# Turning the first quarter of the next norm's rows with a transposing DMA instead of TensorE, at the end of three feed-forward blocks

## The chip, the cores and the metric

The kernel runs on one core of a Trainium2 chip. The metric is device time in microseconds (us) of one execution, the median of several runs. The profile is of one further execution, taken by the hardware profiler.

## The reference

A two-layer encoder over 512 tokens with 1024 channels, float32 throughout. Each layer is a half-step feed-forward block, a mixer, and a second half-step feed-forward block; a final norm follows.

```python
def swiglu(x, w_in, w_out):
    gu = x @ w_in
    g, u = jnp.split(gu, 2, axis=-1)
    return (jax.nn.silu(g) * u) @ w_out
...
    for l in range(DEPTH):
        x = x + 0.5 * swiglu(rms_norm(x, ffn1_norm[l]), ffn1_w_in[l], ffn1_w_out[l])
        x = x + mixer(rms_norm(x, mix_norm[l]), mix_w_in[l], mix_gate_bias[l], na_rpb[l],
                      na_w_out[l], f_w_out[l], mix_w_o[l])
        x = x + 0.5 * swiglu(rms_norm(x, ffn2_norm[l]), ffn2_w_in[l], ffn2_w_out[l])
    return rms_norm(x, final_norm)
```

`D_FF` is 2816. The mixer is neighbourhood attention and a 2-D Fourier transform, gated and summed; the change does not touch it.

## The kernel before

The residual `x` stays in SBUF with tokens on the partitions: 4 blocks of 128 tokens by 1024 channels. Every matrix product is made in split precision: each operand is written as a high part (`whi`, `xh`, `c1h`, ...) and a low remainder (`wlo`, `xl`, `c1l`, ...), and three matmuls replace one: high by high (line 508 of `late_low`), low activation by high weight (line 509), and high activation by low weight (line 511). The high part is an ACT copy, the low part a DVE subtraction that needs that copy: `split` (lines 321 and 322) does this for activations, `Item.prep` (lines 191 and 194) for weights. The products of a block are arranged in Strassen's manner, with seven products numbered m = 1 to 7, so that sums of weight blocks are wanted as well as the blocks themselves.

**Weights.** They come from DRAM as granules of 128 by 1024 float32 (512 KB). `Raw.load` issues the load on SP's queue (line 148) into one of 9 buffers named `raw`; where a sum of two granules is wanted, either a second DMA on GpSimd's queue adds the other granule to it on the way (line 150, `accum_op`), or DVE adds two resident granules (`summed`, line 164). A `raw` buffer comes free once its `wlo` is written. `whi` and `wlo` have three buffers each; `Stream` prepares two granules ahead of the one in use and fetches eight ahead.

**The end of a feed-forward block.** `stage_ffn` first makes the gated hidden activations, turns them to channel-major tiles `at`, and then goes through the output product in 21 steps, i = 0 to 20: m = 1 for three chunks c of the hidden width (i = 0 to 2), m = 2 (i = 3 to 5), then m = 5, 6, 7, 3 for c = 0 (i = 6 to 9), for c = 1 (i = 10 to 13) and for c = 2 (i = 14 to 17), then m = 4 (i = 18 to 20). A step has two weight granules and 18 (c = 0) or 24 matmuls of 512 columns into tiles named `o`. `make(i)` prepares a step's activations: for m = 5, 6, 7 and 4 a DVE combination of two `at` tiles (line 750), then `split`. Step i calls `make(i + 1)` before its product and `make(i + 2)` behind it. At the last chunk of an m, `update` (line 756, DVE) adds the product to `x`, and `squares` (line 375, ACT) sums the squares for the next norm.

**The next norm's rows.** The next stage wants `x` turned: channels on partitions, in high and low parts `xh` and `xl`, plus the gained raw values `xr`. This is done in four quads (i, j): i is the half of the channels, j the half of the tokens. `Norm.quad` does one of them: eight TensorE transposes of 128 by 128 into two PSUM tiles `tr` (line 413), four ACT copies out of PSUM that apply the norm's gain (line 416), one ACT copy for the high part (line 417) and one DVE subtraction for the low part (line 418). Quad (0, 0) is called at step i = 6, once m = 2 has finished that quarter of `x`; the quads (1, 1) and (0, 1) follow at i = 18. This holds for the three feed-forward blocks that are not the last one. The next stage begins with quad (0, 0).

**The other way to turn.** The gated activations are turned without TensorE: `apart` copies a float32 tile as two planes of 16-bit words (`zs`, two ACT copies, line 346) and issues one transposing DMA `zt <- zs` on SP's queue (line 347); `joined_words` puts the words together again (two ACT copies, line 356). Tiles `zs`, `zt`, `xr`, `at` and the split activations share one pool, `slot`, of 23 buffers of 4 KB per partition.

Each engine executes its instructions in order. The order in which instructions go to each queue comes from a scheduler at build time that follows the program's order as priority; only where the code says `manual_schedule` is it the written one. Steps i = 6 to 17 are not under such a block.

Of the kernel before, what the change touches and what calls it, by code (L numbers as in the profile page):

```python
# [9 lines left out]
F32 = mybir.dt.float32  # L10
# [4 lines left out]
AF = mybir.ActivationFunctionType  # L15
# [5 lines left out]
T = 512  # L21
# [69 lines left out]
def encoder_kernel(  # L91
# [3 lines left out]
    V, S, G, PE = nc.vector, nc.scalar, nc.gpsimd, nc.tensor  # L95
# [11 lines left out]
    def nm(s):  # L107
        uid[0] += 1
        return f"{s}_{uid[0]}"

    def slot(dt=F32, s="k", shape=(4, 256)):
        return kp.tile([P, *shape], dt, tag="k", name=nm(s), bufs=23)
# [8 lines left out]
    def pair(s="ps"):  # L121
        return [bank(s), bank(s)]


    x = cp.tile([P, TB, D], F32, tag="x", name="x")
# [146 lines left out]
    class Stream:  # L272
# [32 lines left out]
        def next(self, ahead=AHEAD):  # L305
            self.prep(self.pos + 1 + ahead)
            it = self.items[self.pos]
            self.pos += 1
            return it.out

    ws = Stream()
# [7 lines left out]
    def split(hi, lo, src, scale=None):  # L319
        if scale is None:  # L320
            S.activation(hi, src, AF.Copy)
            V.tensor_tensor(lo, src, hi.bitcast(F32), ALU.subtract)
            return
        S.activation(hi, src, AF.Copy, scale=scale)
        V.scalar_tensor_tensor(lo, src, scale, hi.bitcast(F32), ALU.mult, ALU.subtract)
# [15 lines left out]
    def apart(z):  # L341

        s, t = slot(U16, "zs", (2, 4, 2, P)), slot(U16, "zt", (2, 4, 256))
        words = z.bitcast(U16).rearrange("p b (q f h) -> p h q b f", q=4, h=2)
        for h in range(2):
            S.activation(s[:, h], words[:, h], AF.Copy)  # L346
        nc.sync.dma_start_transpose(
            out=t.rearrange("p h q (b t) -> p (h q b) t", b=2), in_=s.rearrange("p h q b f -> p (h q b f)")
        )
        return t  # L350

    def joined_words(to, t):

        to = to.bitcast(U16).rearrange("p i (t w) -> p w i t", w=2)
        for w in range(2):
            S.activation(to[:, w], t[:, w], AF.Copy)  # L356

    class Norm:
# [39 lines left out]

        def quad(self, i, j):
            self.quad_high(i, j)()  # L400

        def quad_high(self, i, j):

            self.tiles(i)
            js = slice(j * 256, (j + 1) * 256)
            hq, lq = self.h[i][:, :, js], self.l[i][:, :, js]
            raw = self.raw[i, j] = slot(F32, "xr")
            for k2 in range(2):
                tr = bank("tr").rearrange("p (a b) -> p a b", a=2)
                for k in range(2):  # L410
                    d = (4 * i + 2 * k2 + k) * P
                    for b in range(2):
                        PE.transpose(tr[:, k, b * P : (b + 1) * P], x[:, 2 * j + b, d : d + P], ident)
                for k in range(2):
                    kt = 2 * k2 + k
                    S.activation(raw[:, kt, :], tr[:, k, :], AF.Copy, scale=self.gain(4 * i + kt))
            S.activation(hq, raw, AF.Copy)
            return lambda: V.tensor_tensor(lq, raw, hq.bitcast(F32), ALU.subtract)
# [156 lines left out]
    def snap(ps):  # L575
        t = slot(F32, "sn", (2, T))
        for b in range(2):
            S.activation(t[:, b, :], ps[b], AF.Copy)  # L578
        return t
# [35 lines left out]
    def stage_ffn(norm, nxt, late):  # L615
# [25 lines left out]
        raw = norm.raw  # L641
# [24 lines left out]
        if first:  # L666
            for g in range(2):
                w = ws.next()
# [103 lines left out]
        def make(i):  # L772
            if i < len(steps) and i not in made:
                m, c, f = steps[i]
                made[i] = hl(f(), c, f"c{m}")
# [95 lines left out]
        for jb in range(0 if first else 1, NB):  # L871
            f0 = 2 + 4 * jb
            if first and jb == 0:
                with tc.manual_schedule(engines={mybir.EngineType.DVE, mybir.EngineType.Activation}):
                    pa = pair("A")
                    product(pa, acts[1], K4, True)
                    for j in range(2):
                        t = snap(pcl[j])
# [39 lines left out]
        for i, (m, c, _) in enumerate(steps):  # L918
            make(i)
            if i:  # L920
                make(i + 1)
            key = {6: 1, 4: 7}.get(m, m)
            if key not in ps:
                ps[key] = pair(f"o{key}")
            if m == 4 and c == 0 and nxt.mix:
                make(i + 2)
                ws.finish_stage()
                swap_pools(1)
            product(
                ps[key], made.pop(i), list(range(len(CHUNK[0][c]))), c == 0 and m in (1, 2, 3, 5, 7), c == 2,  # L930
                m in (4, 6), by_block=late and i == len(steps) - 1,
            )
            if i == 0:
                settle_at()
            if i == 2:
                turned.reverse()
                joined()
            if i == 5:
                joined()
            if m == 4 and c == 0 and not late:  # L940
                with tc.manual_schedule(engines={mybir.EngineType.DVE, mybir.EngineType.Activation}):
                    make(i + 2)
                    nxt.quad(1, 1)
                    if nxt.mix:
                        nxt.low01 = nxt.quad_high(0, 1)
                    else:
                        nxt.quad(0, 1)
            make(i + 2)
            if i == 6 and not late:
                nxt.quad(0, 0)  # L950
            if m == 4 and c == 1:
                update(ps[1], 1, 0, 1)
            if m == 4 and c == 0 and late:
                gf[0] = slot(F32, "gf", (D,))
                nc.sync.dma_start(out=gf[0], in_=bass.AP(tensor=gfin.tensor, offset=gfin.offset, ap=[[0, P], [1, D]]))
            if c < 2:
                continue
            if m == 1:
                update(ps[1], 0, 0, -1)
            elif m == 2:  # L960
                update(ps[2], 0, 0, 1)
                nxt.squares(0, 0)
            elif m == 5:
                update(ps[5], 0, 1, 1)
                update(ps[5], 1, 1, -1)
            elif m == 6:
                update(ps[1], 1, 1, 1)
            elif m == 7:
                update(ps[7], 1, 1, 1)
                nxt.squares(1, 1)  # L970
                update(ps[1], 0, 1, -1)
            elif m == 3:
                update(ps[3], 0, 1, 1)
                nxt.squares(0, 1)
                if late:
                    make(i + 3)
            elif late:
                with (
                    tc.issue_after(ws.items[-1].last.ins),
                    tc.manual_schedule(engines={mybir.EngineType.DVE, mybir.EngineType.Activation}),  # L980
                ):
                    ready = nxt.inverses(2)
                    next(ready)
                    gained(2, 0)
                    next(ready)
                    gained(2, 1)
                    for _ in ready:
                        pass
                    scaled(nxt, 2)
                    update(ps[7], 1, 0, 1, (0,))  # L990
                    nxt.squares(1, 0, (0,))
                    root = [nxt.inverse(b, *nxt.terms(b)) for b in range(2)]
                    next(root[0])
                    gained(3, 0)
                    gained(3, 1)
                    scaled(nxt, 3)
                    update(ps[7], 1, 0, 1, (1,))
                    nxt.squares(1, 0, (1,))
                    next(root[1])
                    next(root[0])  # L1000
                    gained(0, 0)
                    next(root[0])
                    gained(0, 1)
                    scaled(nxt, 0)
                    next(root[1])
                    next(root[1])
                    whole(nxt, 1, 0)
                    whole(nxt, 1, 1)
            else:
                update(ps[7], 1, 0, 1)  # L1010
                if not nxt.mix:
                    nxt.squares(1, 0)
                nxt.later((1, 0))
# [797 lines left out]
    def swap_pools(kind, fetch=True):  # L1811

        if scope[0]:
            scope[0].close()
        scope[0] = ExitStack()
        name = nm("stage")
        scope_pool[0] = scope[0].enter_context(tc.tile_pool(name=name, bufs=1, reuse_waits="tile"))
        if kind:
            mix_pool[0] = scope_pool[0]
            raw_pool[0] = mix_raw  # L1820
        else:
            raw_pool[0] = ffn_raw
        if fetch:
            ws.enter(ws.stage + 1)
# [16 lines left out]
    for l in range(L):  # L1841
        nxt = Norm(3 * l + 1)
        stage_ffn(norm, nxt, False)
        norm, nxt = nxt, Norm(3 * l + 2)
        stage_mixer(l, norm, nxt)
        norm, nxt = nxt, Norm(3 * l + 3)
# [141 lines left out]
```

## Time and profile before

| | us |
|---|---|
| three runs | 1858.61, 1860.62, 1858.87 |
| median | 1858.87 |
| the profiled execution | 1859.64 |
| its span, first to last instruction | 1857.9 |

Between the span and the execution's own time lie 1.7 us, before the first and behind the last instruction. TensorE's granted clock was 0.999 of full speed. The profile names matmuls PE and weight loads into the array PEld; a matmul's end is modelled and overlaps the next one's start, so the distance between starts (0.227 us for 512 columns) says more than a matmul's own duration (0.389 us).

The output products of the three blocks that the change touches begin at 220.6, 821.7 and 1142.2 us of the trace and are called block A, B and C below.

### The profile page before, as it was taken

How to read it: one execution, taken by the hardware profiler on the slowest of the kernel's cores; microseconds unless marked ns; L12 is line 12 of the kernel's file. 1: busy time of each engine (PE TensorE's matmuls, PEld its weight loads, DVE VectorE, ACT ScalarE, POOL GpSimd, SP SyncE). 2: the span in 40 equal slices, each digit the busy share in tenths (PEclk: the TensorE clock that was granted, in tenths of full speed). 3: DMA queues.
4: the chain of work that ended last, by engine and by line, in shares of the span. 5: the costliest groups of instructions: out<-in, count | busy, mean ns of one | idle time of the engine just before them, and what ended most of it. 6: DMA issues, size and time to landing. Idle time of an engine off the chain costs nothing.

```text
span 1857.9 us, 24616 instructions
## 1 busy us (share of the span) xinstructions
PE 1842.2 (99%) x8862; PEld 1530.1 (82%) x8862; DVE 1605.6 (86%) x1950; ACT 1311.2 (71%) x1780; POOL 171.3 (9%) x210
## 2 busy tenths in 40 slices
PE   9999999999999999999999999999999999999997
PEld 7888878888888888888888888888888888888886
DVE  7878899786889987889998888998869899887898
ACT  6777875668676767777666778766675776777865
POOL 0001011100111010001010100101001101010010
PEclk9999999999999999999999999999999999999999
DMA  9898799932896788879888887988249867888794
GB/s 301 222 240 219 188 255 277 216 118 86 248 230 183 180 224 223 216 199 263 253 200 217 225 216 198 268 278 212 69 150 237 227 174 178 234 210 215 211 280 145
DMA packets 198458, 394.21 MB, mean 212 GB/s; under 512 B 103808, under 2 KB 103936, under 8 KB 198336
## 3 DMA queue, kind: packets, MB, share of 16 engines
q1 hardware_dynamic: 169664, 294.30, 49.2%
q0 software_dynamic: 28528, 98.33, 29.7%
q8 instruction: 69, 1.13, 0.3%
q14 instruction: 53, 0.43, 0.1%
q10 hardware_dynamic: 144, 0.02, 0.0%
HBM read 365.85 MB, written 2.11 MB: 198 GB/s over the span
## 4 chain that ended last, share of the span: by engine, by line
PE 88%; DVE 6%; DMA 2%; issue 2%; ACT 1%; SPq 0%; DVEq 0%; ACTq 0%
PE A L508 10%; PE A L511 10%; PE A L509 10%; PE B L509 5%; PE B L508 5%; PE B L511 5%; PE o L511 5%; PE o L509 5%; PE o L508 4%; PE ps L315 4%; PE ps L316 3%; PE ps L317 3%; PE C L508 3%; PE C L509 3%; PE C L511 3%
## 5 line engine op out<-in xcount | busy, mean ns | idle before, releaser
L194 DVE TENSOR_TENSOR wlo<-raw,whi 128x1024 fp32r<-128x1024 f32 (+1 forms) x534 | 632.0, 1195 | 172.8 <-ACT whi L191 171.3
L191 ACT ACTIVATE whi<-raw 128x1024 fp32r<-128x1024 f32 (+1 forms) x534 | 546.0, 1033 | 253.5 <-DVE raw L164 56.9
L150 POOL DMA_DIRECT2D raw<-in_wst_dram x166 | 144.2, 887 | 1339.3 <-DMA raw<-in_wst_dram 596.8
L164 DVE TENSOR_TENSOR raw<-raw,raw 128x1024 f32<-128x1024 f32 (+1 forms) x150 | 179.2, 1195 | 2.0
L509 PE MATMUL A<-whi,xl 128*128 128x512 f32 x400 | 155.7, 389 | 0.0
L508 PE MATMUL A<-whi,xh 128*128 128x512 f32 x400 | 155.7, 389 | 0.0
L356 ACT ACTIVATE at<-zt 128x1024 uint16<-128x1024 uint16 (+2 forms) x96 | 111.0, 1168 | 20.9 <-DMA zt<-zs 20.9
L186 ACT ACTIVATE whi<-raw 128x1024 fp32r<-128x1024 f32 (+1 forms) x83 | 85.9, 1035 | 46.9 <-issue 12.5
L511 PE MATMUL A<-wlo,xh 128*128 128x512 f32 x400 | 115.0, 389 | 0.0
L187 DVE SCALAR_TENSOR_TENSOR wlo<-raw,whi 128x1024 fp32r<-128x1024 f32 (+1 forms) x83 | 98.4, 1195 | 11.3 <-ACT whi L186 11.0
L511 PEld LDWEIGHTS A<-wlo,xh 128*128 128x128 f32 x400 | 75.1, 188 | 15.6
L508 PEld LDWEIGHTS A<-whi,xh 128*128 128x128 f32 x400 | 75.1, 188 | 15.4
L509 PEld LDWEIGHTS A<-whi,xl 128*128 128x128 f32 x400 | 75.1, 188 | 15.4
L508 PE MATMUL C<-whi,xh 128*128 128x512 f32 x208 | 81.1, 390 | 0.5 <-ACT whi L191 0.5
L509 PE MATMUL C<-whi,xl 128*128 128x512 f32 x208 | 81.0, 389 | 0.0
L509 PE MATMUL B<-whi,xl 128*128 128x512 f32 x208 | 81.0, 389 | 0.0
L508 PE MATMUL B<-whi,xh 128*128 128x512 f32 x208 | 80.9, 389 | 0.0
L730 ACT ACTIVATE th<-sn,rh 128x512 f32<-128x512 f32 x80 | 55.1, 715 | 36.2 <-DVE sn L583 35.4
L346 ACT ACTIVATE zs<-th 128x1024 uint16<-128x1024 uint16 x80 | 79.5, 1042 | 0.9 <-DVE th L737 0.9
L578 ACT ACTIVATE sn<-A 128x512 f32<-128x512 f32 x104 | 59.0, 584 | 24.9 <-PE A L511 24.9
L511 PE MATMUL B<-wlo,xh 128*128 128x512 f32 x208 | 59.8, 389 | 0.0
L511 PE MATMUL C<-wlo,xh 128*128 128x512 f32 x208 | 59.8, 389 | 0.0
(438 smaller groups left out, 4681.5 us busy)
## 6 DMA issues: line engine op xcount, KB each, us to landing
raw<-in_wst_dram SPq DMA_DIRECT2D x470, 512.0 KB, 5.7
raw<-in_wst_dram POOLq DMA_DIRECT2D x174, 512.0 KB, 8.0
raw<-in_wst_dram SPq DMA_DIRECT2D x30, 256.0 KB, 3.8
bm<-in_bias_dram SPq DMA_DIRECT2D x16, 384.0 KB, 3.5
x<-in_xin_dram SPq DMA_DIRECT2D x4, 512.0 KB, 10.2
raw<-in_wst_dram POOLq DMA_DIRECT2D x8, 256.0 KB, 8.4
dft<-in_dft_dram POOLq DMA_DIRECT2D x8, 256.0 KB, 4.3
gb<-in_gbias_dram SPq DMA_DIRECT2D x4, 512.0 KB, 14.8
```

Source lines behind the costliest of these rows:

```text
L150: G.dma_start(out=self.t, in_=wst[GRAN_AT[self.plus]][:, 0 : self.n], accum_op=ALU.add)
L164: V.tensor_tensor(self.raw.t, self.raw.t, self.add.t, ALU.add)
L186: S.activation(hi, t, AF.Copy, scale=-1.0)
L187: self.last = V.scalar_tensor_tensor(lo, t, -1.0, hi.bitcast(F32), ALU.mult, ALU.subtract)
L191: S.activation(hi[:, cs], t[:, cs], AF.Copy)
L194: self.last = V.tensor_tensor(lo[:, cs], t[:, cs], hi[:, cs].bitcast(F32), ALU.subtract)
L315: PE.matmul(ps, lh, rh, start=start, stop=False, skip_group_check=again)
L346: S.activation(s[:, h], words[:, h], AF.Copy)
L356: S.activation(to[:, w], t[:, w], AF.Copy)
L508: PE.matmul(ps, lh, rh, start=start, stop=False, skip_group_check=again)
L509: PE.matmul(ps, ll, rh, start=False, stop=False, skip_group_check=again)
L511: PE.matmul(ps, lh, rl, start=False, stop=stop, skip_group_check=again)
```

## The change

In these three blocks, quad (0, 0) is no longer made by `Norm.quad`. At step i = 6 the new `quad_apart` calls `apart` on that quarter of `x` (two ACT copies, one transposing DMA on SP's queue). The rest is a generator whose five pieces run at the ends of steps i = 9 to 13: one word plane joined, the other joined, two gain scalings, two gain scalings, and `split` (ACT copy and DVE subtraction).

```diff
-    def joined_words(to, t):
+    def joined_words(to, t, ws=(0, 1)):
 
         to = to.bitcast(U16).rearrange("p i (t w) -> p w i t", w=2)
-        for w in range(2):
+        for w in ws:
             S.activation(to[:, w], t[:, w], AF.Copy)
...
+        def quad_apart(self, i, j):
+
+            t = apart(x[:, 2 * j : 2 * j + 2, i * T : (i + 1) * T])
+
+            def rest():
+                self.tiles(i)
+                js = slice(j * 256, (j + 1) * 256)
+                raw = self.raw[i, j] = slot(F32, "xr")
+                for w in range(2):
+                    joined_words(raw, t, (w,))
+                    yield
+                for k in range(4):
+                    S.activation(raw[:, k, :], raw[:, k, :], AF.Copy, scale=self.gain(4 * i + k))
+                    if k % 2:
+                        yield
+                split(self.h[i][:, :, js], self.l[i][:, :, js], raw)
+                yield
+
+            return rest()
...
             if i == 6 and not late:
-                nxt.quad(0, 0)
+                rest00 = nxt.quad_apart(0, 0)
+            if 9 <= i <= 13 and not late:
+                next(rest00)
```

## The prediction

> **What bounds the kernel now.** I read the page's totals first, then the waits of TensorE, then the timeline of each engine around the transposes in block A.
>
> ```profile
> span 1857.9 us, 24616 instructions
> PE 1842.2 (99%) x8862; PEld 1530.1 (82%) x8862; DVE 1605.6 (86%) x1950; ACT 1311.2 (71%) x1780; POOL 171.3 (9%) x210
> ...
> PE 88%; DVE 6%; DMA 2%; issue 2%; ACT 1%; SPq 0%; DVEq 0%; ACTq 0%
> ```
>
> Over the span TensorE is the bound: it is busy 99% of the time and carries 88% of the chain that ended last. But 6% of that chain is DVE and 2% DMA, and a mean over the span says nothing of the three stretches in question. TensorE's timeline does:
>
> ```profile
> 256.12 0.39 PE L511 MATMUL o<-wlo,c5h 128*128 128x512 f32 x1
> 256.35 1.03 PE L413 MATMUL tr<-ident,x 128*128 128x128 f32 x8
> 257.14 0.48 PE L508 MATMUL o<-whi,c6h 128*128 128x512 f32 x1
> 257.45 0.39 PE L509 MATMUL o<-whi,c6l 128*128 128x512 f32 x1
> ...
> 264.97 0.50 PE L511 MATMUL o<-wlo,c7h 128*128 128x512 f32 x1 [0.31 <-DVE wlo L194]
> ...
> 310.55 1.20 PE L511 MATMUL o<-wlo,c3h 128*128 128x512 f32 x4 [0.22 <-DVE wlo L194]
> 911.91 0.50 PE L511 MATMUL o<-wlo,c3h 128*128 128x512 f32 x1
> 1230.73 1.19 PE L511 MATMUL o<-wlo,c3h 128*128 128x512 f32 x4 [0.32 <-DVE wlo L194]
> ```
>
> The eight transposes stand at the end of step i = 6. The matmul of 257.45 would stand at 256.35 + 0.23 = 256.58 without them, so they cost 0.87 us of TensorE, 2.6 us in three blocks. Behind them TensorE runs into DVE: at step i = 17 (m = 3, c = 2) the first matmul that reads `wlo` waits 0.22 us in block A and 0.32 us in block C for DVE to write it. In block B there is no wait, but hardly any room either, as DVE's timeline shows:
>
> ```profile
> 263.10 1.22 DVE L418 TENSOR_TENSOR xl<-xr,xh 128x1024 fp32r<-128x1024 f32 x1
> 264.24 0.68 DVE L194 TENSOR_TENSOR wlo<-raw,whi 128x512 fp32r<-128x512 f32 x1
> ...
> 281.83 1.23 DVE L194 TENSOR_TENSOR wlo<-raw,whi 128x1024 fp32r<-128x1024 f32 x1 [0.42 <-ACT whi L191]
> 881.19 1.23 DVE L194 TENSOR_TENSOR wlo<-raw,whi 128x1024 fp32r<-128x1024 f32 x1 [1.10 <-PE o L511]
> 910.62 1.23 DVE L194 TENSOR_TENSOR wlo<-raw,whi 128x1024 fp32r<-128x1024 f32 x1
> 1202.01 1.23 DVE L194 TENSOR_TENSOR wlo<-raw,whi 128x1024 fp32r<-128x1024 f32 x1 [0.77 <-ACT whi L191]
> ```
>
> The `wlo` of 910.62 ends at 911.85 and is read at 911.91: 0.06 us. The windows below give DVE 41.58 busy us of 42 in block A, 36.87 of 38 in B and 39.23 of 40 in C; nearly all the missing time is the one wait per block in the rows above, at i = 12. What stands behind that wait is in the chain and the windows:
>
> ```profile
> 268.93 1.14 DVE wlo L194
> ...
> 270.53 10.10 DMA raw<-in_wst_dram
> ...
> 280.74 1.07 ACT whi L191
> 1191.07 9.75 DMA raw<-in_wst_dram
> 1200.92 1.07 ACT whi L191
> ```
>
> ```profile
> 258.00:300.00 42.00, 41.69 (x184) 33.97 (x183) 41.58 (x39) 25.91 (x30) 5.87 (x7) 1.00 1.03 296
> 860.00:898.00 38.00, 38.00 (x169) 31.47 (x168) 36.87 (x35) 23.25 (x25) 5.16 (x6) 1.00 1.04 303
> 1180.00:1220.00 40.00, 40.00 (x178) 33.14 (x177) 39.23 (x37) 24.57 (x26) 5.49 (x7) 1.00 1.04 299
> 300.00:304.00 4.00, 4.00 (x19) 3.34 (x18) 4.00 (x7) 1.06 (x1) 0.00 (x0) 1.00 0.11 44
> 266.00:272.00 6.00, 6.00 (x28) 4.97 (x27) 6.00 (x7) 3.04 (x3) 1.72 (x2) 1.00 1.00 399
> 231.95:234.20 2.25, 2.25 (x11) 1.88 (x10) 2.25 (x3) 0.76 (x1) 0.69 (x1) 1.00 1.22 273
> ```
>
> Columns: stretch, length, busy time of PE, PEld, DVE, ACT, POOL with counts, clock, DMA share, GB/s. From step 7 to about step 15 the 16 DMA engines are busy without a break (1.03, 1.04, 1.04), and right behind it they fall to 0.11. A summing load on GpSimd's queue that is issued at 270.53 takes 10.1 us to land, and the high part that ACT makes of it starts 0.11 us later. So the last wait in this stretch goes DMA, ACT, DVE, TensorE, and TensorE has no spare to give or take: the weights set the pace.
>
> **The change part by part.** For each block:
>
> *TensorE's transposes.* Minus 0.87 us of TensorE. It is not on the path at i = 17: TensorE would only come earlier to the same wait for `wlo`. I count 0.
>
> *DVE's subtraction for `xl`.* It stays one instruction, and moves from step 8 (263.10) to step 13 or a little later, past the wait at i = 12 but still ahead of i = 17. It takes 264.24 - 263.10 = 1.14 us. DVE comes to i = 12 that much sooner, and is that much later again at i = 17. If the load behind the wait comes 1.14 us sooner too (in the chain above it is released by DVE's `wlo` of 268.93, which comes sooner), the move costs 0; if the load's landing is set by full DMA engines, DVE only waits 1.14 us longer and the move costs 1.14. I take 0, since the chain names DVE as what released that DMA.
>
> *The transposing DMA.* Rows for its parts (for a group: min, median, max in ns, or busy us and mean ns):
>
> ```profile
> 257.57 1.55 ACT L416 ACTIVATE xr<-tr,gn 128x256 f32<-128x256 f32 x4
> 229.30 3.47 SPq L347 DMA_TRANSPOSE zt<-zs  x1
> L346 ACT ACTIVATE zs<-th 128x1024 uint16<-128x1024 uint16 x80 | 79.5, 1042 | 0.9 <-DVE th L737 0.9
> L356 ACT ACTIVATE at<-zt x96: 477/1358/1384, 83.9 to 1766.6; 128x1024 uint16<-128x1024 uint16 x64, 128x256 uint16<-128x256 uint16 x16, 128x768 uint16<-128x768 uint16 x16
> L416 ACT ACTIVATE xr<-tr,gn 128x256 f32<-128x256 f32 x80 | 31.0, 473 | 0.0
> DMA to landing us min/median/max: 4.3/5.5/8.9
> ```
>
> The two `zs` copies of 1.04 us take the place of the copies that began at 257.57, so the DMA is issued on SP's queue at some 259.6 in block A, and its data moves inside the full stretch. `zt` is 128 x 4 KB = 0.52 MB. The one that was issued at 229.30 is the main traffic of the window 231.95 to 234.20, just ahead of its landing some 5.5 us after issue, and that window ran at 273 GB/s: 0.52 MB at that rate is 1.92 us of all 16 engines. In a stretch with no free DMA time this is added in full to what lands later, up to the idle 300 to 304, so to the summing load that DVE waits for at i = 12. Bounds: 0 if the engines have room after all, 1.92 if not. Nearest are the windows of the stretch itself, share 1.03 and more; I take 1.92. On SP's own queue the weight loads behind it wait while it is issued, 3.47 us in the row; they are early enough otherwise and I count nothing more for them here.
>
> The Trainium skill (Perfetto Trace Analysis, Identifying the Most-Contended Engine, with the peak of Engine Utilization) says to judge DMA by memory bandwidth against 358 GB/s, not by how busy the 16 engines look. By that rule 296 to 303 GB/s leaves a sixth free and the transposing DMA, which reads no DRAM, costs 0. The trace speaks against it here: a window of the same stretch moved 399 GB/s, above that figure, while the stretch's mean is lower at the same share, so bytes do not say how full the engines are.
>
> *ACT.* Out go four copies from PSUM of 0.47 us (1.55 us together, as they overlap); in come two `zs` copies (2.1), two joining copies (1.36 us each, the median, less 0.1 of overlap) and four scalings of 128x256, for which 0.47 us each (L416) is the nearest row, 1.55 together. The high part stays. Net 4.7 us per block, on an engine with 16 us free of 42 in the window. The five pieces of 1.36, 1.36, 0.8, 0.8 and 1.07 us come behind `make(i + 2)`, where ACT idles ahead of the next weight copy:
>
> ```profile
> 268.96 1.06 ACT L321 ACTIVATE c6h<-at 128x1024 fp32r<-128x1024 f32 x1 [1.93 <-DVE at L750]
> 275.86 2.08 ACT L191 ACTIVATE whi<-raw 128x1024 fp32r<-128x1024 f32 x2 [1.40 <-PE o L511]
> 280.74 2.02 ACT L191 ACTIVATE whi<-raw 128x1024 fp32r<-128x1024 f32 x2 [1.85 <-DMA raw<-in_wst_dram]
> 285.45 2.01 ACT L191 ACTIVATE whi<-raw 128x1024 fp32r<-128x1024 f32 x2 [1.75 <-DVE raw L164]
> ```
>
> Gaps of 1.40 to 1.93 us hold pieces of up to 1.36. I count 0; if a piece falls just ahead of a weight copy that DVE waits for, up to 1.36 us each. The first joining copy waits for the transposing DMA; behind it on ACT's queue stand the weight copies of step 10. With some 5.5 us to landing (median of 44) the DMA lands near 265 and the copy comes at 269: covered by about 4 us.
>
> *Two more tiles* (`zs`, `zt`) live in the pool of 23. By the code 12 `at`, three pairs of split activations, one `xr` and these two make 21: no wait.
>
> Sum per block: 0 + 0 + 1.92 + 0 = 1.92 us, less 0.06 of room in block B: 3 x 1.92 - 0.06 = 5.7 us. The profiled execution took 1859.64 (span 1857.9), so it would take 1865.3; it lies 0.77 above the median of the three runs, 1858.87, and from that median I forecast **1864.6 us**. With nothing of the 1.14 kept the sum is 3 x 3.06 - 0.06 = 9.1 us, 1868.0. Both ends belong to this case.
>
> **The rivals.**
>
> *Hidden transfer, DVE the bound.* The DMA engines have room, or the plain loads that are early take the delay and the summing load is not late. Then DVE has the same work as before in the same stretch and ends it at the same time: the 0.87 us of TensorE become a longer wait at i = 17, and the result is no change, 1858.9, give or take 1. For it speak the 399 GB/s above the mean of 296, and the two separate queues (GpSimd for summing loads, SP for the transposing DMA). Against it the 0.11 us between landing and use.
>
> The Trainium skill (DMA: Bandwidth & Descriptors, Queues, rings and completion order) says that each DMA engine takes packets in turn from its queues. By that rule a summing load loses at most half of the 1.92 us, 0.96 per block and 2.9 us in all, 1861.7: between this rival and the forecast, and within this rival's chance. No view of this profile parts the two queues inside a window.
>
> *Not slower, a gain (the other side).* The scheduler puts `xl` on DVE's queue behind the `wlo` of i = 17. Then DVE is 1.14 us sooner there, and TensorE keeps its 0.87 and loses some of its waits. It decides at the order of DVE's queue alone: A and C give up to 1.14 each, B 0.87: 3.15 us, 1855.7. Against it: in block A `xl` came one and a half steps (6 us) behind its transposes, and from step 13 (292 us) that is 298, well ahead of 310.
>
> *A late transpose.* SP's queue waits for `zs`, or the DMA is queued behind weight loads, and the joining copy at i = 9 holds ACT with the weight copies behind it. The waits view has
>
> ```profile
> ACT at L356 <- DMA zt<-zs: 20.9, 10, 4.3
> SPq L347 <- ACT whi L191: 127.8, 20, 14.2
> ```
>
> ten such waits of 2.1 us on average, 4.3 at most, and SP held for 6.4 us on average with loads behind it. At 2.1 us per block it adds 6.3 to the forecast, 1870.9; at 4.3 it adds 12.9, 1877.5.
>
> **How the numbers follow.** The forecast case, 1861.5 to 1868.0, gets 0.48; the hidden transfer 0.28; the gain 0.12; the late transpose 0.12. No change that a measurement of this kernel can tell means within 0.2%, 3.7 us: 1855.2 to 1862.6. The gain of 1855.7 lies inside that, so faster by over 0.2% gets only 0.05, for an order of the queues that none of this foresees. Within 0.2% are the hidden transfer (0.28), the rest of the gain (0.07) and the lower end of the forecast case (0.04): 0.39. Slower by over 0.2%: 0.44 + 0.12 = 0.56. The range reaches from 1856.5, inside the gain, to 1872.5, past the late transpose at its mean; some 0.08 is left out below and 0.08 above.
>
> **What would show it.** Right: in the changed profile the transposes of lines 413 are 136 and not 160; DMA share stays over 1.0 from step 7 and its end moves some 2 us later against the block's start; the DVE wait at i = 12 grows from 0.42, 1.10 and 0.77 us, and the TensorE wait at i = 17 grows from 0.22, 0 and 0.32 to 2 us and more. Hidden transfer: the wait at i = 17 grows by just 0.9 us, that at i = 12 by no more than 1.1. Gain: `xl` stands behind i = 17. Late transpose: ACT idles for `zt` at i = 9. The forecast is wrong if the blocks A, B and C do not get longer.

## The result and the profile after

| kernel | median, us | runs, us | ratio to before (95% interval) |
|---|---|---|---|
| before | 1858.93 | 1858.61 to 1861.68, 6 runs | |
| after | 1873.54 | 1870.31 to 1880.40, 6 runs | 1.0084 (1.0067 to 1.0100) |

The change makes the kernel 14.6 us slower. The forecast was 5.7 us slower, and 1873.54 lies 1.0 us above the range. The profiled execution of the changed kernel took 1871.83. Its page, in the lines that the prediction showed of before (line 528 now stands where 508 stood, 529 for 509, 531 for 511, 770 for 750):

```profile
span 1870.1 us, 24593 instructions
PE 1845.2 (99%) x8838; PEld 1525.9 (82%) x8838; DVE 1606.3 (86%) x1950; ACT 1324.8 (71%) x1792; POOL 171.0 (9%) x210
PE 85%; DVE 7%; DMA 3%; issue 2%; ACT 2%; SPq 0%; POOL 0%; DVEq 0%; ACTq 0%; POOLq 0%
```

The totals hardly move. In the chain that ended last, 3 points go from PE to DVE, DMA and ACT. TensorE's timeline tells where. These are the first matmuls of the blocks A, B and C and of the last one in the changed kernel:

```profile
220.62 0.39 PE L528 MATMUL o<-whi,c1h 128*128 128x512 f32 x1
...
825.69 0.39 PE L528 MATMUL o<-whi,c1h 128*128 128x512 f32 x1
...
1149.97 0.39 PE L528 MATMUL o<-whi,c1h 128*128 128x512 f32 x1
...
1753.97 0.39 PE L528 MATMUL o<-whi,c1h 128*128 128x512 f32 x1
```

and the last one before:

```profile
1742.35 0.39 PE L508 MATMUL o<-whi,c1h 128*128 128x512 f32 x1
```

Before, A, B and C began at 220.6, 821.7 and 1142.2. So the lag is nothing at A, then 4.0, 7.8 and 11.6 us: each stretch that holds one of the three blocks loses 3.8 to 3.9 us, alike, and what comes ahead of block A loses nothing. Inside the blocks the largest stall is at step i = 12 (after's timeline; the bracket is the idle time ahead and what ended it):

```profile
280.45 1.06 ACT L191 ACTIVATE whi<-raw 128x1024 fp32r<-128x1024 f32 x1 [4.24 <-DMA raw<-in_wst_dram]
281.53 1.23 DVE L194 TENSOR_TENSOR wlo<-raw,whi 128x1024 fp32r<-128x1024 f32 x1 [4.03 <-ACT whi L191]
281.55 0.50 PE L528 MATMUL o<-whi,c7h 128*128 128x512 f32 x1 [1.89 <-ACT whi L191]
...
886.14 0.50 PE L528 MATMUL o<-whi,c7h 128*128 128x512 f32 x1 [1.90 <-ACT whi L191]
...
1209.52 0.50 PE L528 MATMUL o<-whi,c7h 128*128 128x512 f32 x1 [1.23 <-ACT whi L191]
```

ACT waits for a summing load, DVE and TensorE wait for ACT's `whi`. What changed ahead of that stands 22 us earlier, on SP's queue. After:

```profile
258.13 7.35 SPq L347 DMA_TRANSPOSE zt<-zs  x1
265.58 0.52 SPq L148 DMA_DIRECT2D raw<-in_wst_dram  x1
...
862.02 6.63 SPq L347 DMA_TRANSPOSE zt<-zs  x1
868.75 1.53 SPq L148 DMA_DIRECT2D raw<-in_wst_dram  x1
...
1186.32 6.72 SPq L347 DMA_TRANSPOSE zt<-zs  x1
```

and before, the same weight load in block A:

```profile
259.74 0.33 SPq L148 DMA_DIRECT2D raw<-in_wst_dram  x1
```

SP is held 6.6 to 7.4 us by the issue of one transposing DMA, and in block A the weight load behind it goes out at 265.58 instead of 259.74. A summing load on GpSimd's queue starts only when the plain load under it has landed, so it is late too. That is in the chain after, in order of time:

```profile
266.21 4.54 DMA raw<-in_wst_dram
...
272.59 11.33 DMA raw<-in_wst_dram
...
284.03 1.07 ACT whi L191
```

The weight load issued at 266.21 releases GpSimd. Its summing load of 271.37 (269.18 before) lands at 280.34 and ends ACT's wait of 4.24 us; the next one, of 272.59 (270.53 before), lands 11.3 us later, and ACT's `whi` of 284.03 follows. The theory was then: **the loss is the weight loads' delay behind the transfer** (theory Q), from SP's hold, from the transfer's time on the full DMA engines, or both. The rival (L): the moved low half or the pieces on ScalarE cost it.

### The profile page after: what moved, and what is told of

It reads as the page before. It is cut to its first block, busy times and chain, and to the rows that moved or that the text cites. A ratio compares the mean times of both kernels' runs of the same rounds, so it can differ in the third digit from the quotient of the medians.

```text
span 1870.1 us, 24593 instructions
## 1 busy us (share of the span) xinstructions
PE 1845.2 (99%) x8838; PEld 1525.9 (82%) x8838; DVE 1606.3 (86%) x1950; ACT 1324.8 (71%) x1792; POOL 171.0 (9%) x210
## 4 chain that ended last, share of the span: by engine, by line
PE 85%; DVE 7%; DMA 3%; issue 2%; ACT 2%; SPq 0%; POOL 0%; DVEq 0%; ACTq 0%; POOLq 0%
PE A L528 10%; PE A L531 10%; PE A L529 10%; PE B L529 5%; PE B L531 5%; PE B L528 5%; PE o L531 4%; PE o L529 4%; PE o L528 4%; PE ps L315 4%; PE ps L316 3%; PE ps L317 3%; DVE wlo L194 3%; PE C L529 3%; PE C L531 3%; PE C L528 3%
## 5 line engine op out<-in xcount | busy, mean ns | idle before, releaser
L531 PEld LDWEIGHTS A<-wlo,xh 128*128 128x128 f32 x400 | 75.1, 188 | 15.6
## 6 DMA issues: line engine op xcount, KB each, us to landing
gb<-in_gbias_dram SPq DMA_DIRECT2D x4, 512.0 KB, 15.9
```

The lines of the kernel that those rows point to most:

```text
L531: PE.matmul(ps, lh, rl, start=False, stop=stop, skip_group_check=again)
```

## The experiments

Medians are of 4 to 12 executions; the kernel before, executed beside them, had 1858.7 to 1860.4 us. "Per block" is the difference of the ratios times 1860 us, divided by three. In these units the interval of one ratio reaches some 0.6 to 1 us to each side (1.5 for the transfer on ScalarE's queue and for the two halves), that of a difference of two ratios some 1 to 1.3.

**Which part costs.** Four kernels: the change without its transfer, the transfer without the change, the transfer as a plain DMA, and the low half alone.

The first, in `quad_apart`:

```diff
-            t = apart(x[:, 2 * j : 2 * j + 2, i * T : (i + 1) * T])
+            s = slot(U16, "zs", (2, 4, 2, P))
+            words = x[:, 2 * j : 2 * j + 2, i * T : (i + 1) * T].bitcast(U16).rearrange("p b (q f h) -> p h q b f", q=4, h=2)
+            for h in range(2):
+                S.activation(s[:, h], words[:, h], AF.Copy)
+            t = s.rearrange("p h q b f -> p h q (b f)")
```

> The changed kernel without the transposing DMA: the four pieces read the copies of the rows themselves (the data are not turned, so the quarter's values are other ones). All else stays: 24 transposes fewer on TensorE, the copies on ScalarE spread over five steps, the low half at i=13. Theory Q (the transfer costs by what stands behind it on SP's queue and on the DMA engines): the wait at i=12 falls back to that of before, about 0.4 to 1.1 us a block, and with it the 3.3 to 3.8 us a block; time 1858 to 1860 us, and down to 1856.5 if the removed transposes are worth their 0.87 us a block. Rival L (the low half moved to i=13, or the pieces on ScalarE, cost it): the blocks stay 3 us longer, 1868 to 1872 us.

Measured 1861.61 us, ratio 1.0008 (0.9997 to 1.0020). The second, on the kernel before:

```diff
             if i == 6 and not late:
                 nxt.quad(0, 0)
+                apart(x[:, 0:2, 0:T])
```

> The kernel before with one thing added: at i=6 of the three blocks a quarter of the rows is also copied and turned by a transposing DMA, and nothing reads the result; TensorE's transposes, the copies out of PSUM and the place of the low half are those of before. Theory Q: the loss of the change appears without the rest of it, 1869 to 1873 us, with the wait at i=12 for whi. The prediction's own term (only the full DMA engines' time, 1.92 us a block): 1864.6 us. Rival L (low half or pieces): 1858.9 to 1860 us, with what the copies on ScalarE cost.

Measured 1870.61 us, 1.0058 (1.0046 to 1.0070). The third is the first with a tile `t` of its own and

```diff
+            nc.sync.dma_start(out=t.rearrange("p h q b -> p (h q b)"), in_=s.rearrange("p h q b f -> p (h q b f)"))
```

> The changed kernel with the transposing DMA replaced by a plain one, of the same 0.52 MB from the same tile to the same tile, on the same queue (the data are not turned, so the quarter's values are other ones). Theory Q1 (SP is held for 6.6 to 7.4 us while it issues the transposing DMA, and the weight loads behind it go out late): a plain DMA is issued in about 0.3 us, the loads behind it go out as before, and most of the loss goes: 1859 to 1862 us. Theory Q2 (what costs is the engines' time for the bytes): 0.52 MB at the 399 GB/s of full engines are 1.3 us a block, 1862.8 us or more, with the loads landing late while issued early. Rival L: 1868 to 1872 us.

Measured 1865.78 us, 1.0032 (1.0020 to 1.0044). The fourth:

```diff
             if i == 6 and not late:
-                nxt.quad(0, 0)
+                low00 = nxt.quad_high(0, 0)
+            if i == 13 and not late:
+                low00()
```

> The kernel before with the subtraction of the quarter's low half moved from i=6 to i=13 in the three blocks, and nothing else. Theory Q: VectorE waits for whi at i=12 in any case and the summing takes up what is freed, within 1 us of before, 1857.9 to 1859.9 us. Rival L: 1.14 us a block on the path of VectorE from i=12 to i=17, 1862.3 us.

Measured 1862.62 us, 1.0010 (1.0001 to 1.0020).

So L falls: all of the change but the transfer costs 1.5 us in three blocks, with an interval from -0.6 to 3.7, and the low half alone 1.9. The transfer alone costs 10.8 of the whole change's 15.6 (0.0084 x 1860). What is left between them lies within the intervals; part of it may be that the scheduler put the transfer behind three more weight loads, as SP's rows of that kernel show. The next load then went out at 268.93, and in the kernel before at 264.95:

```profile
261.69 7.15 SPq L347 DMA_TRANSPOSE zt<-zs  x1
268.93 0.53 SPq L148 DMA_DIRECT2D raw<-in_wst_dram  x1
```

The plain transfer of the same 0.52 MB was issued in 0.55 us and let the next load out at 259.50:

```profile
258.40 0.55 SPq L408 DMA_DIRECT2D zt<-zs  x1
259.50 0.33 SPq L148 DMA_DIRECT2D raw<-in_wst_dram  x1
```

It costs 1.5 us a block over the kernel without a transfer (0.0024 x 1860 / 3), near the 1.3 us of 0.52 MB at 399 GB/s. The transposing one costs 4.7 (0.0076). The bytes are the same, so they do not explain the 3.2 us between the two. Two things differ. One is the time for which SP is held. The other is the packets in which the DMA engines move the data: by the totals of the DMA queue, three transposing transfers add 6240 packets to the 169664 of the kernel without one, and three plain ones add 432. The packet records of the changed kernel hold 2048 packets of 256 bytes for each transfer, and their times add up to 3.76, 3.65 and 3.43 us of all 16 engines in the blocks A, B and C. The plain one's 128 packets of 4 KB, at the 0.16 to 0.18 us of such packets in that stretch, come to some 1.3 to 1.4 us (an estimate).

**The hold of SP by itself.** The kernel without the transfer, with many DMAs of 8 bytes in its place (20, 12 and 9 of them):

```diff
+            d = slot(U16, "zt", (2, 4, 2, P))
+            for k in range(20):
+                nc.sync.dma_start(out=d[0:1, k % 2, k // 2 % 4, 0, 4 * k : 4 * k + 4], in_=s[0:1, k % 2, k // 2 % 4, 0, 4 * k : 4 * k + 4])
```

> The kernel without the transposing DMA (pieces read the copies themselves, so the quarter's values are other ones), with twenty DMAs of 8 bytes each in its place on SP: at 0.33 us of issue each they hold SP for about 6.6 us, and move nothing to speak of. Theory Q1 (the hold of SP makes the larger part, 1873.5 less 1865.8, some 7.8 us in three blocks): 1866 to 1869 us, with the weight loads behind issued at about 265 us instead of 259 and the wait at i=12 on whi. Theory Q2 (what costs is the engines' time for bytes and packets, and the loads behind SP's hold would have queued anyway): 1859 to 1862.5 us, as without the transfer.

> As with the twenty DMAs of 8 bytes, but twelve: they were issued every 0.61 us, twenty held SP for 12.3 us and cost 8.6 us a block, so twelve hold it for 7.4 us, as long as the transposing DMA does (7.35 us in the first block), still with no bytes to speak of (the pieces read untransposed copies, so the quarter's values are other ones). Theory Q1 (the hold of SP is the larger part; what exceeds about 3.7 us of it is paid): 3.7 us a block, 1870 to 1873 us. Theory Q2 (the bytes and packets are what costs, a hold of this length is covered): 1860 to 1863 us.

> As with the twelve DMAs of 8 bytes, but nine. Twelve held SP until 267.4 us and twenty until 270.4 (no transfer: the next weight load went out at 259.07); they cost 4.2 and 7.9 us a block over the kernel without the transfer. Nine should let the next weight load out at 264 to 265.6 us, about where the transposing DMA lets it out (265.58). Sum theory (hold and engines' time add up): by the slope of those two runs the hold is worth some 1 to 2.1 us a block, 1864.5 to 1868 us, and the rest of the changed kernel's loss is the engines' time. Hold-only theory (the loads behind are late by the hold and bytes add nothing): 1872 to 1875 us, as the changed kernel. The pieces read untransposed copies, so the quarter's values are other ones.

Measured 1886.20 us, 1.0135 (1.0122 to 1.0148); 1873.30, 1.0076 (1.0063 to 1.0088); and 1866.61, 1.0041 (1.0028 to 1.0055). SP's rows in block A, with twenty, twelve and nine:

```profile
257.48 12.91 SPq L411 DMA_DIRECT2D zt<-zs  x20
270.48 0.39 SPq L148 DMA_DIRECT2D raw<-in_wst_dram  x1
```

```profile
257.44 9.95 SPq L411 DMA_DIRECT2D zt<-zs  x12
267.48 0.39 SPq L148 DMA_DIRECT2D raw<-in_wst_dram  x1
```

```profile
256.38 6.27 SPq L411 DMA_DIRECT2D zt<-zs  x9
262.85 0.34 SPq L148 DMA_DIRECT2D raw<-in_wst_dram  x1
```

A held SP costs time though nothing to speak of is moved. Twelve held it longer than meant (9.95 us, not 7.4), and nine shorter, so the fair measure is how much later the first weight load behind goes out. Counted from the start of each block, mean of three, over the kernel without a transfer (38.63, 37.32 and 36.89 us after the start):

| in place of the transfer | next load out, us after block start (A, B, C) | later by | cost per block over no transfer |
|---|---|---|---|
| nine | 43.27, 43.03, 41.19 | 4.9 | 2.0 |
| twelve | 47.16, 44.31, 42.69 | 7.1 | 4.2 |
| twenty | 50.27, 47.86, 48.24 | 11.2 | 7.9 |
| the transposing DMA (after) | 44.97, 43.06, 43.18 | 6.1 | 4.7 |

Each microsecond past some 2.9 us is paid nearly in full. Twenty's price has another part, however. Around TensorE's waits of 5.3 to 5.8 us its granted clock was 0.50 for some 6.8 us in each block, as in block A (the last three columns are the clock, the DMA share and GB/s); twelve and nine show 3.4 us of this in one block of three, the changed kernel none inside the blocks:

```profile
283.80:290.60 6.80, 3.94 (x9) 3.14 (x10) 1.31 (x2) 2.63 (x4) 1.70 (x2) 0.50 1.05 292
```

Between nine and twelve, 6.1 us are worth 3.2 a block; with 1.5 for the plain transfer that makes 4.7, the measured loss. That this sum fits does not show that the loss parts so. These are windows of block A inside the hold, first in the changed kernel, then with twelve and with twenty:

```profile
258.00:266.00 8.00, 8.00 (x37) 6.64 (x36) 8.00 (x10) 5.79 (x8) 0.68 (x1) 1.00 1.06 178
```

```profile
264.00:268.00 4.00, 4.00 (x19) 3.27 (x18) 4.00 (x5) 1.49 (x2) 0.00 (x0) 1.00 0.22 41
```

```profile
264.00:270.00 6.00, 6.00 (x27) 4.90 (x27) 6.00 (x7) 3.08 (x3) 0.00 (x0) 1.00 0.11 19
```

With twelve and twenty small DMAs the 16 engines ran dry, for want of loads. While the transposing DMA held SP they stayed full (1.06, and 1.03 in the blocks B and C), and fewer bytes moved: 667 packets of that window are under 512 bytes. So in block A the first load behind it went out 5.84 us later than in the kernel before and landed just 2.0 us later (269.48 for 267.52).

Hold and packets overlap: 3.2 for a hold and 3.6 for the packets would be 6.8, more than was lost. Hold alone fits less well than the sum, as it would give nine, which let the load out 1.2 us sooner, 4.7 - 1.2 = 3.5 a block, a ratio of 1.0064, and their interval ends at 1.0055; but the 4.7 has an interval too, and by the spans of the profiled executions (1865.4 with nine, 1870.1 after) nine are just 1.6 a block cheaper, so it is not excluded. What is shown is that a hold alone can cost time here, and that the packets took the engines' time. How the loss parts between the two stays open.

**Other ways to issue it.** On ScalarE's queue:

```diff
-    def apart(z):
+    def apart(z, queue=None):
...
-        nc.sync.dma_start_transpose(
+        (queue or nc.sync).dma_start_transpose(
...
-            t = apart(x[:, 2 * j : 2 * j + 2, i * T : (i + 1) * T])
+            t = apart(x[:, 2 * j : 2 * j + 2, i * T : (i + 1) * T], nc.scalar)
```

> The changed kernel with the transposing DMA of the quarter issued by ScalarE instead of SP; nothing else changes. SP is not held, ScalarE is, for as long as the issue takes (7.35 us on SP in the first block), ahead of its share of the weights of the next steps. Theory Q1: the weight loads go out as before and what is left is the engines' time, 1.4 us a block as with the plain transfer up to the prediction's 1.92: 1864 to 1866 us, if ScalarE can make up its hold (it waits 4.24 us for a raw sum at 280 us). Theory Q2 (engines' time of the transposing packets themselves, 3.3 us and more a block): 1870 to 1874 us.

Measured 1886.08 us in five executions (a sixth took 1911.43), 1.0130 (1.0105 to 1.0156), worse than either theory had it. The profile is of the sixth, so its rows show where the hold went and not what it costs in the median:

```profile
258.34 10.31 ACTq L347 DMA_TRANSPOSE zt<-zs  x1
268.78 0.63 ACT L191 ACTIVATE whi<-raw 128x512 fp32r<-128x512 f32 x1 [9.51 <-issue]
```

```profile
269.46 0.80 PE L528 MATMUL o<-whi,c7h 128*128 128x512 f32 x1 [6.45 <-ACT whi L191]
```

The hold, 10.31 us there, moved to ACT's queue, where `whi` for the very next steps stands behind it. In the blocks B and C of that profile the transfer took 31.5 and 28.3 us to land, which stays unexplained. This tells nothing of the packets' share; it shows that the queue which issues the transfer is held, ACT's as well as SP's.

In two halves, one at i = 6 and one at i = 8 (each plane of `zs` its own DMA):

```diff
+            turn(0)
...
+                turn(1)
+                yield
                 raw = self.raw[i, j] = slot(F32, "xr")
...
-            if 9 <= i <= 13 and not late:
+            if 8 <= i <= 13 and not late:
```

> The changed kernel with the transposing DMA cut in two of half the size, one at i=6 and one at i=8 (about 8 us later on TensorE); same bytes, same packets. Theory Q1 (a hold costs what exceeds about 3.7 us): each half holds SP for 3.3 to 3.7 us, which is covered, and only the engines' time is left, 1.4 to 1.92 us a block: 1864 to 1866.5 us. Theory Q2 (bytes and packets cost, however they are issued): 1870 to 1874 us as with the whole one.

Measured 1886.61 us, 1.0138 (1.0115 to 1.0162). The scheduler put the second half right behind the first, so this did not test two short holds:

```profile
256.22 7.43 SPq L410 DMA_TRANSPOSE zt<-zs  x2
```

Together they hold SP as long as the whole one in block A (7.43 us), and for less in block C (4.42), yet this costs 10 us more than the change. The packets differ: the halves took 15.9 us from issue to landing in block A, the whole one 10.0,

```profile
zt<-zs SPq DMA_TRANSPOSE x2, 15.9
```

and the same 2048 packets took 7.31, 5.47 and 6.99 us of all 16 engines in the three blocks, nearly twice as long as in the changed kernel. ACT's waits for raw sums were longer, 4.95 us at 272.38 and 6.20 at 284.89, and TensorE's clock fell to 0.50 three times for 3.4 us. Why the packets of two halves take longer stays open. But the engines' time follows the loss where the hold does not: from the start of block A to that of the last output product in the profiles, over the kernel without a transfer, the plain transfer costs 1.8 us a block for some 1.4 of engines' time, the whole transposing one 3.4 for 3.6, and the two halves 8.4 for 6.6. This speaks for the packets as the larger share; it does not part them from the hold.

**The same transfer at another place.** In the kernel before, SP issues nothing between these two loads, and the DMA engines fall idle:

```profile
296.71 0.34 SPq L148 DMA_DIRECT2D raw<-in_wst_dram  x1
303.65 0.33 SPq L148 DMA_DIRECT2D raw<-in_wst_dram  x1
```

First the whole change moved there:

```diff
-            if i == 6 and not late:
+            if i == 14 and not late:
                 rest00 = nxt.quad_apart(0, 0)
-            if 9 <= i <= 13 and not late:
+            if 16 <= i <= 20 and not late:
                 next(rest00)
```

> The changed kernel with the quarter's copies and transposing DMA moved from i=6 to i=14, and the five pieces from i=9 to 13 to i=16 to 20, so that the transfer is issued about 40 us later, near the few microseconds of each block (304 to 308 in the changed kernel's first block) in which the DMA engines are idle. Theory Q (the loss is that of loads behind the transfer, on SP's queue and on the engines, while both are full): the wait at i=12 goes back to before's and most of the loss with it, 1858 to 1863 us; what may be late instead is the update after i=20, which the pieces on ScalarE now stand beside. If the transfer's time on the engines is paid wherever it falls, 1863 to 1866 us; if the hold of SP is paid wherever it falls, 1870 us or more.

Measured 1862.66 us, 1.0011 (1.0002 to 1.0020): most of the loss is gone. With the pieces a step earlier (15 to 19):

> The kernel with the transfer at i=14, but its five pieces at i=15 to 19 instead of 16 to 20. In the run with 16 to 20 the transfer stood in a stretch in which SP has nothing to issue, the wait at i=12 was gone, and 1.9 us were lost after the first and third block, where the next stage's first product waited for the quarter's xh, split in the last piece. Theory Q (place decides): those 3.8 us go as well, and with TensorE's 0.87 us a block less it comes to 1856 to 1860 us. Rival (any transfer costs 1.4 us a block, the last piece only hid it): 1862 to 1864 us.

Measured 1866.19 us, 1.0033 (1.0021 to 1.0045). With the last two pieces inside the hand-ordered part of i = 18:

```diff
                         nxt.quad(0, 1)
+                    for _ in rest00:
+                        pass
```

> The kernel with the transfer at i=14, the first three pieces at i=15 to 17 and the last two (two scalings, the split) inside the hand-ordered part of i=18, so that the quarter's xh can't be put off to the end of the block, as it was at 330 us with the pieces at 15 to 19 and at 16 to 20. Theory Q: the 1.9 us after the first and the third block go, 3.8 us less than the 2 to 6 us over before of those two runs: 1857 to 1862 us. Rival (the added work on ScalarE at i=18 makes whi late in i=18 to 20): 1862 to 1866 us, with waits for whi between 313 and 331 us.

Measured 1873.60 us, 1.0067 (1.0055 to 1.0080). Both moves missed. ACT's and TensorE's rows, first with the pieces at 15 to 19, then with the hand-ordered part:

```profile
329.80 1.10 ACT L321 ACTIVATE xh<-xr 128x1024 fp32r<-128x1024 f32 x1
330.95 0.49 PE L528 MATMUL A<-whi,xh 128*128 128x512 f32 x1 [1.01 <-ACT xh L321]
332.33 0.50 PE L529 MATMUL A<-whi,xl 128*128 128x512 f32 x1 [0.88 <-DVE xl L322]
```

```profile
334.16 0.80 PE L528 MATMUL A<-whi,xh 128*128 128x512 f32 x1 [3.83 <-ACT xh L321]
335.42 0.79 PE L529 MATMUL A<-whi,xl 128*128 128x512 f32 x1 [0.46 <-DVE xl L322]
```

Around the waits of 3.83 us, behind block A and again behind block C, the granted clock was 0.50 for some 6.8 us, so such a wait costs more than its own length. The next stage begins with this quad. Whatever stands in the program behind the hand-ordered part of i = 18 comes behind it on ACT's queue, and what is put at its end comes last of all. So all pieces have to stand ahead of i = 18: the same work in three pieces, at i = 15, 16 and 17 (shown against the version with 16 to 20).

```diff
                     joined_words(raw, t, (w,))
-                    yield
+                    if w == 0:
+                        yield
...
-                    if k % 2:
+                    if k == 1:
                         yield
...
-            if 16 <= i <= 20 and not late:
+            if 15 <= i <= 17 and not late:
```

> The kernel with the transfer at i=14 and the work of the five pieces in three, at i=15 to 17: one joining copy; the other and two scalings; two scalings and the split. With pieces behind i=18 ScalarE reached the split at 329.8 and 333.1 us, behind the copies and scalings that the hand-ordered part of i=18 puts on its queue, and the next stage waited 1.9 and 4.3 us for it. Theory Q (place on the queues decides): the split comes at about 315 us, the next stage waits for nothing, and the time is that of the transfer alone at i=14 (1858.6) less up to 0.87 us of transposes a block: 1856 to 1860 us. Rival (ScalarE has no room at i=15 to 18): whi late between 305 and 320 us, 1861 to 1866 us.

Measured 1858.86 us, 0.9999 (0.9990 to 1.0008). `xh` is made at 312.69 and the next stage does not wait for it:

```profile
312.69 1.04 ACT L321 ACTIVATE xh<-xr 128x1024 fp32r<-128x1024 f32 x1
```

The transfer held SP for 6.00 us in block A of this kernel, from 294.40 on, and it cost nothing: the next load went out 81.5 us after the block's start, in the kernel before 83.1 us after it.

Last, the transfer alone, unused, at i = 14 in the kernel before:

> The kernel before with only the copies and the transposing DMA added at i=14, their result unused (at i=6 the same addition made 1870.6 us). Theory Q (place on SP's queue decides: in the kernel before SP has nothing to issue from 297.3 to 303.65 us): 1859 to 1862 us. If engines' time or hold are paid wherever they fall: 1864 us, or 1870 us.

Measured 1858.64 us, 0.9988 (0.9979 to 0.9997). At i = 6 the same line had cost 10.8 us. Its rows:

```profile
299.20 2.93 SPq L347 DMA_TRANSPOSE zt<-zs  x1
303.07 0.34 SPq L148 DMA_DIRECT2D raw<-in_wst_dram  x1
```

The issue fits into SP's gap, and the load behind it goes out at 303.07, where before it went out at 303.65. This ratio, the lowest of all, has an interval that ends at 0.9997, and it belongs to a kernel that only does more than the one before. So 2 us cannot be told from no change here, and no version is shown to beat the kernel before.

## Why the prediction was wrong

*TensorE's transposes, counted 0.* No run speaks against it: with them gone and no new wait (three pieces at i = 15 to 17) the time is that of before.

*`xl`, counted 0, bounds 0 to 1.14 us a block.* 0.6 a block (1.9 us in three) when moved alone, with an interval from nearly 0 to 1.2; the spread just named leaves open whether it is more than 0.

*ACT's pieces, counted 0.* Right: with the moved `xl` they cost 1.5 us in three blocks, with an interval that holds 0. The transfer landed at 268.15, 3 us after the 265 that it was given, and the first joining copy came at 271.78 without a wait.

*The transposing DMA, 1.92 us a block and no more.* This is the step that failed. Its mechanism, that the transfer's time on full DMA engines is passed on to what lands later, fits the traces; its size does not. The 1.92 us were the transfer's bytes at the rate of one window, 231.95 to 234.20, and no row gave the time of its packets among other loads. The packet records of the changed kernel give 3.76, 3.65 and 3.43 us of all 16 engines, and its blocks lost 3.8 to 3.9 us each. With 3.6 in place of 1.92, and 0.6 for `xl`, the same sum would be 3 x 4.2 - 0.06 = 12.5 us against 14.6 measured. The last sentence of that term failed as well: that the weight loads behind the transfer on SP's queue are early enough, "and I count nothing more for them". The first of them went out 6.1 us later (mean of the three blocks). The issue was taken as 3.47 us from a row at 229.30; in the full stretch it took 6.6 to 7.4, and the transposing DMAs of the kernel before already ranged from 1.36 to 6.83. And the slack of those loads was asserted, not read: in the kernel before, the summing load waits for the plain load under it and was itself used 0.11 us after landing. The small DMAs put such a hold at some 3.2 us a block by itself; how much of that is in the loss here, on top of the packets' time, stays open.

*The rivals.* The time fell into the case of the late transpose (1870.9 to 1877.5), which for the number is luck: SP was held with loads behind it, as that case has it, but the joining copy, which was to carry the price, waited for nothing. The hidden transfer is refuted at i = 6, and true at i = 14. Its rule from the Trainium skill (Perfetto Trace Analysis, Identifying the Most-Contended Engine), that engines' busy time says less than memory bandwidth, would have a transfer that reads no DRAM cost nothing; the plain one, which reads none, cost 4.5 us in three blocks, so here the busy share was the better guide.

*What was to show it.* The transposes became 136, and the idle stretch of the DMA engines, 300 to 304 before, is now 304 to 308; in 300 to 304 their share is 0.73 for 0.11 (columns as in the prediction's windows):

```profile
258.00:302.00 44.00, 41.54 (x177) 32.16 (x176) 38.75 (x37) 28.65 (x33) 5.78 (x7) 1.00 1.05 289
304.00:308.00 4.00, 4.00 (x19) 3.31 (x18) 4.00 (x6) 0.72 (x1) 0.00 (x0) 1.00 0.02 6
```

DVE's wait at i = 12 grew to 4.03 us in block A. TensorE's wait did not come at i = 17, where 2 us and more were named, but at i = 12, for `whi`; at i = 17 it was 0.68:

```profile
313.83 1.20 PE L531 MATMUL o<-wlo,c3h 128*128 128x512 f32 x4 [0.68 <-DVE wlo L194]
```

Open remain how the loss parts between SP's hold and the packets' time, why the packets of two halves take longer, and why the changed kernel's runs spread over 10 us.

## What to carry to other kernels

A DMA has two prices: its time on the engines, which goes by its packets and not by its bytes alone, and the time for which it holds the queue that issues it. Read both from records of the same kind of transfer in a stretch as full as the one where it will stand, and list what is issued behind it, to the load that is used as soon as it lands. A test that puts a stand-in for one price has to show the same load on the engines, as the small DMAs here did not. Then look for the gap in which that queue has nothing to issue: the same transfer cost 10.8 us at one step and nothing eight steps on. Work that feeds the next stage must stand ahead of any hand-ordered part on its queue.

## What the runs showed of the hardware that was not expected

The time that a transposing DMA of 0.52 MB holds its queue is not fixed: 2.93 us as the engines fell idle, 3.47 at 229 us, 6.63 to 7.35 in the full stretch on SP, 10.31 on ScalarE's queue; a plain DMA of that size held SP 0.55 us in the same stretch. Its engines' time is not that of a plain one either: 3.43 to 3.76 us for 2048 packets of 256 bytes in the full stretch, against some 1.4 (an estimate from 128 packets of 4 KB). The Trainium skill (Perfetto Trace Analysis, DMA Instruction — HWDGE (DVE, Sync)) has the issuing sequencer occupied until all descriptors are generated, and the DMA engines starting before that when there are more than the buffer holds. The trace agrees: in block A of the changed kernel the first packet moved at 261.98, with the hold from 258.13 to 265.48. The rows above add that the hold was longer where the engines were fuller. The Trainium skill (DMA: Bandwidth & Descriptors, Issuing engines are not separate DMA queues) calls the time to initiate a DMA usually small relative to the DMA itself; here it was 7.35 us of the 10.0 from issue to landing:

```profile
zt<-zs SPq DMA_TRANSPOSE x1, 10.0
```

Waits of TensorE went with a lower granted clock: 0.50 for some 6.8 us around the five waits of 3.83 to 5.81 us with twenty small DMAs and with the hand-ordered part, and for 3.4 us around some shorter ones. Around the waits of 1.23 to 1.90 us in the changed kernel it stayed at 1.00.
